# Two operands in one tile in a transformer FFN's down product, and the output projection's weight loads ordered ahead

## The chip, the core and the metric

The program runs on one core of one Trainium2 chip. A core has five engines that work side by side, each on its own queue of instructions: TensorE (PE, matrix products, with its weight loads shown as PEld), VectorE (DVE), ScalarE (ACT), GpSimd (POOL) and SyncE (SP), whose queue here issues most of the transfers between HBM and the on-chip memory SBUF. Products land in PSUM, a small memory of eight banks.

The metric is the device time of one execution in microseconds (us). The profile is of one execution; the times are of others.

## The reference, cut to what matters

A trunk of two layers on 1024 tokens of width 1024 in float32. The first layer mixes tokens by attention, the second by a recurrence; each then has a gated FFN of inner width 2816.

```python
x = x + mix
h = rms_norm(x, norm_ffn[layer])
x = x + swiglu(h, ffn_w_gate[layer], ffn_w_up[layer], ffn_w_down[layer])

def swiglu(h, w_gate, w_up, w_down):
    return (jax.nn.silu(h @ w_gate) * (h @ w_up)) @ w_down
```

The change touches the last product of the FFN, `(...) @ w_down`, in both layers, and in the attention layer the projection at the end of the mix, `concatenate([out_a, out_b]) @ w_out`, where `out_b` is a softmax-weighted sum of three attention patterns.

## The kernel before

**Float32 products from rounded parts.** TensorE multiplies a rounded form of float32 here. Each operand is split into a high part, written by ScalarE (a CAST), and a low part, source minus high part, written by VectorE: `split`, L153 and L154. A product of two operands is three matmuls, high by high, high by low and low by high.

**The FFN's down product** (`ffn_down`, from L893) is cut into blocks by Strassen's scheme in Winograd's form: the tokens in two halves of 512, the output columns in two halves of 512, the inner 2816 in two halves of 11 blocks of 128 (`N` is 11). The eight products of halves become seven, each a sum over `f` of 0 to 10. In the order of the program they are: the first and the second (plain operands), then the fifth and the sixth together, whose operands are sums of loaded blocks, then the third, the seventh and the fourth. One `f` of one product is two operands of 128 x 512 (a block of activations `act`, loaded from HBM, and one of `w_down`), two splits, and 12 matmuls (`add`, L932): four groups of 128 tokens, three matmuls each.

Before the change each operand has a tile of its own: `load` (L907 to L909) takes one of 12 `raw` tiles of 128 x 512 and issues one transfer; `halves` splits activations into `as` and weights into `ws`, five tiles of each. The blocks that the second product loads are kept in `s2[f]` and `t2[f]`; the fifth and sixth overwrite them with their own operands, which the third, seventh and fourth use again.

For each `f` of the fifth and sixth: GpSimd adds two activation blocks (L977), subtracts the kept weights from new ones (L978) and, after the split of the fifth's operands, subtracts the kept activations (L980); VectorE subtracts once (L981). Then the results, the sixth's operands, are split. TensorE takes the sixth's 12 matmuls of `f` after the fifth's 12 of `f + 1`.

In the third, seventh and fourth GpSimd makes one subtraction for each `f` (L993, L998, L1004) and in the seventh VectorE makes one more (L999). `to` (L938) adds a finished bank of PSUM to the residual.

**The output projection** (`out_proj`, called for the attention layer first) takes eight weight blocks `w[k]` for each half of the columns; each is loaded and split by `load_split` (the transfer is L168), with two `raw` tiles. Between the matmuls of blocks 0, 1 and 2 the program runs a part of `merge`: the first part reads the attention's statistics (L586) and a selector (L599) and turns them into weights of the three patterns; the other two load the patterns' outputs `oB` (L622), multiply them by those weights on VectorE (L625), add them on GpSimd (L627) and split the sum into the activations that the last two weight blocks need. The outputs of the last pattern are written to `oB` by GpSimd's queue (L513).

**What sets the order.** The program text gives dependencies and a priority, not the order of issue. The framework plans each engine's queue by a modelled timeline, in which an instruction is placed when the model has it ready; each engine then runs its queue strictly in that order, waiting where data is late. `after(ins, earlier)` adds an edge that fixes an order of issue and no wait. `seen` uses it to hold TensorE's instructions in the program's order in the projection of the first half of the tokens.

The functions that the diff touches, with what calls them:

Of the kernel before, what the change touches and what calls it, by code (L numbers as in the profile page):

```python
# [122 lines left out]
class Trunk:  # L123
# [144 lines left out]
    def attention(self, hp, mp):  # L268
# [333 lines left out]
        def merge(mp, psum, q, seen):  # L602
# [15 lines left out]
            for pr in range(2):  # L618
                yield
                l = ls[3 * pr:3 * pr + 3]  # L620
                for g in range(3):
                    nc.sync.dma_start(l[g], oB[g, pr][:, q * H:(q + 1) * H])  # L622
                    pb = psum.tile([P, H], F32, name="pb", tag="pd")
                    seen(nc.tensor.matmul(pb, selr[:, (g * 2 + pr) * P:(g * 2 + pr + 1) * P], f, start=True, stop=True))
                    nc.vector.tensor_tensor(l[g], pb, l[g], MUL)  # L625
                    if g:
                        nc.gpsimd.tensor_tensor(l[0], l[0], l[g], ADD)  # L627
                self.split(os2[q][1][:, 2 + pr, 0], os2[q][1][:, 2 + pr, 1], l[0])
# [264 lines left out]
    def ffn_down(self, layer, act, x_src, side, done):  # L893
# [5 lines left out]
        ve, po = nc.vector, nc.gpsimd  # L899
        es = ExitStack()  # L900
        pool = lambda n, b, **k: es.enter_context(TP(tc, name=n, bufs=b, **k))
        pr, xp, ap, bp, pk = (pool(n, 1, side=side) for n in ("dr", "dx", "da", "db", "dk"))
        py, pz = pool("fpa", 4, space=PSUM), pool("fpb", 4, space=PSUM)
        N = NF // 2
        inner = lambda j, f: f if j else N + f

        def load(src, keep=None):  # L907
            r = keep or pr.tile([P, H], F32, name="raw", tag="raw", bufs=12)
            nc.sync.dma_start(r, src)  # L909
            return r  # L910

        def A(q, j, f, keep=None):
            return load(act[inner(j, f), q], keep)

        def B(j, c, f, keep=None):
            return load(a["wd"][layer, inner(j, f)][:, c * H:(c + 1) * H], keep)

        def halves(s, w):
            r = []
            for p, n, z in ((ap, "as", s), (bp, "ws", w)):  # L920
                r.append(p.tile([P, 2, H], F32R, name=n, tag=n, bufs=5))
                self.split(r[-1][:, 0], r[-1][:, 1], z)
            return r

        banks = lambda p: [p.tile([P, H], F32, name="pd", tag="pd") for _ in range(4)]

        def add(ps, f, b, s, w, start):
            t = slice(b * P, (b + 1) * P)
            first = start and f == 0
            pe = nc.tensor.matmul  # L930
            for i, (x, y) in enumerate(((0, 0), (0, 1), (1, 0))):
                pe(ps[b], s[:, x, t], w[:, y], start=first and i == 0, stop=f == N - 1 and i == 2, skip_group_check=True)  # L932

        x = []

# [4 lines left out]
        def product(ps, start, take, ops, mid=None, last=2):  # L940

            end = []
            for f in range(N):
                o = halves(*ops(f))
                if f >= N - last:
                    end.append((f, o))
                    continue
                for b in range(4):
                    add(ps, f, b, *o, start)
                if mid and f == 4:  # L950
                    mid()
            for b in range(4):
                for f, o in end:
                    add(ps, f, b, *o, start)
                take(b)

        def load_x():
# [1 line left out]
                x.append(xp.tile([P, D], F32, name=f"x{b}"))  # L959
                nc.sync.dma_start(x[b], x_src[b * P:(b + 1) * P, :])  # L960

        s2, t2 = ([pk.tile([P, H], F32, name=f"{n}{f}") for f in range(N)] for n in ("s2", "t2"))
        zs, ys = banks(pz), banks(py)
        product(zs, True, lambda b: to(0, 0, zs, b), lambda f: (A(0, 1, f), B(1, 0, f)), load_x)
        product(ys, True, lambda b: to(0, 0, ys, b), lambda f: (A(0, 0, f, s2[f]), B(0, 0, f, t2[f])))
        zs = banks(pz)
        late = []

        def sixth(f, o):
            for b in range(4):  # L970
                add(ys, f, b, *o, False)
                if f == N - 1:
                    to(0, 1, ys, b)

        for f in range(N):
            s1, a22, t1, b22 = A(1, 0, f), A(1, 1, f), B(0, 1, f), B(1, 1, f)
            po.tensor_tensor(s1, s1, a22, ADD)  # L977
            po.tensor_tensor(t1, t1, t2[f], SUB)  # L978
            o5 = halves(s1, t1)
            po.tensor_tensor(s2[f], s1, s2[f], SUB)  # L980
            ve.tensor_tensor(t2[f], b22, t1, SUB)  # L981
            for b in range(4):
                add(zs, f, b, *o5, True)
                if f == N - 1:
                    to(1, 1, zs, b)
            late.append((f, halves(s2[f], t2[f])))
            if len(late) > 1:
                sixth(*late.pop(0))
        sixth(*late.pop())

        def third(f):
            a12, b22 = A(0, 1, f), B(1, 1, f)
            po.tensor_tensor(a12, a12, s2[f], SUB)  # L993
            return a12, b22

        def seventh(f):
            a22, b11 = A(1, 1, f), B(0, 0, f)
            po.tensor_tensor(a22, a22, s2[f], SUB)  # L998
            ve.tensor_tensor(b11, t2[f], b11, SUB)  # L999
            return a22, b11  # L1000

        def fourth(f):
            a22, b21 = A(1, 1, f), B(1, 0, f)
            po.tensor_tensor(b21, b21, t2[f], SUB)  # L1004
            return a22, b21

        def take3(b):
            to(0, 1, zs, b)
# [700 lines left out]
```

## Time and profile before

| what | value |
|---|---|
| time, median of 3 runs | 2815.28 us (2813.53 to 2815.95) |
| the profiled execution, its own time | 2819.46 us |
| span of the profile | 2817.7 us |
| mean granted TensorE clock | 0.963 |
| TensorE busy | 2648.6 us, 94% of the span |
| VectorE busy | 1739.9 us, 62% |
| ScalarE busy | 1198.0 us, 43% |
| GpSimd busy | 1053.6 us, 37% |
| down product of layer 0, first to last matmul | 1046.7 to 1277.1 us |
| down product of layer 1 | 2581.2 to 2807.3 us |
| output projection of layer 0 | 499.1 to 609.5 us |

A busy share is over the whole program. A stage of it can hang on another engine than the rest, so the stages are read one by one: in the views by group, an engine's idle time stands with the instruction that ended it, as `[idle <- releaser]`. "SPq", "POOLq" and the like are the queues that issue transfers. PEclk is the share of its full clock that TensorE was granted.

### The profile page before, as it was taken

The numbers are of one execution on the slowest core, as the hardware profiler recorded it, in microseconds if no ns is written. First come the engines' busy times: TensorE is split into PE (matmuls) and PEld (weight loads), VectorE is DVE, ScalarE is ACT, GpSimd is POOL, SyncE is SP. The second block draws the span as 40 slices with busy tenths as digits, with TensorE's granted clock in tenths as the row PEclk, the third lists the DMA queues.
The fourth block names the chain that finished last, engine by engine and source line by source line (L and its number), as shares of the span: only waits on it lengthen the run. The fifth ranks groups of instructions, "written<-read, shape, count | busy, mean of one in ns | idle before, by whom it ended". The sixth has DMA issues, their size and how long they took to land.

```text
span 2817.7 us, 42321 instructions
## 1 busy us (share of the span) xinstructions
PE 2648.6 (94%) x15526; PEld 2117.2 (75%) x15526; DVE 1739.9 (62%) x2961; ACT 1198.0 (43%) x2387; POOL 1053.6 (37%) x768
## 2 busy tenths in 40 slices
PE   8999998989999999998899889889899999999998
PEld 7777776677888877776677657678877888887776
DVE  4555565566344447888767677766677544444988
ACT  3445446334333333355644454334434333333334
POOL 1221221236434425545444433224444534441644
PEclk9999999999999999999999999888899999999999
DMA  4111112632222237463667588898552322225654
GB/s 140 46 38 46 46 53 73 216 111 82 83 86 86 79 115 254 152 202 112 215 201 206 148 245 214 216 253 247 180 195 86 105 79 87 79 69 204 206 157 161
DMA packets 304751, 392.61 MB, mean 139 GB/s; under 512 B 97928, under 2 KB 167944, under 8 KB 304544
## 3 DMA queue, kind: packets, MB, share of 16 engines
q1 hardware_dynamic: 299568, 375.72, 42.6%
q10 hardware_dynamic: 4496, 12.62, 1.1%
q8 instruction: 122, 2.00, 0.3%
q0 software_dynamic: 480, 1.57, 0.2%
q14 instruction: 85, 0.70, 0.1%
HBM read 281.56 MB, written 108.27 MB: 138 GB/s over the span
## 4 chain that ended last, share of the span: by engine, by line
PE 55%; DVE 14%; DMA 6%; issue 3%; POOL 2%; ACT 1%; SPq 1%; POOLq 0%; DVEq 0%; ACTq 0%
PE y L784 17%; PE z L784 9%; PE pd L932 6%; PE x L784 4%; PE pg L1360 2%; DVE ws L154 2%; DVE as L154 2%; PE pz L180 2%; PE pz L182 2%; PE pz L181 2%; PE o L1474 2%; DMA raw<-in_wd 2%; PE po L180 2%; PE po L181 1%; PE po L182 1%
## 5 line engine op out<-in xcount | busy, mean ns | idle before, releaser
L932 PE MATMUL pd<-ws,as 128*128 128x512 f32 x1848 | 431.9, 395 | 21.4 <-DVE ws L154 20.3
L932 PEld LDWEIGHTS pd<-ws,as 128*128 128x128 f32 x1848 | 350.7, 191 | 100.6 <-DVE ws L154 25.4
L784 PE MATMUL y<-t,cw 128*128 128x512 f32 x1584 | 370.2, 389 | 0.0
L784 PEld LDWEIGHTS y<-t,cw 128*128 128x128 f32 x1584 | 297.3, 188 | 62.4
L154 DVE TENSOR_TENSOR cw<-raw,cw 128x512 fp32r<-128x512 f32 x264 | 213.5, 811 | 201.6 <-ACT cw L154 198.0
L154 ACT CAST cw<-raw 128x512 fp32r<-128x512 f32 x264 | 163.1, 621 | 245.8 <-PE z L784 103.8
L793 POOL TENSOR_TENSOR c<-c 128x512 f32<-128x512 f32 x66 | 111.7, 1692 | 187.7 <-DVE c L800 136.7
L154 ACT CAST wh<-raw 128x512 fp32r<-128x512 f32 (+1 forms) x122 | 93.3, 766 | 173.5 <-PE mm L181 53.6
L180 PE MATMUL mm<-hx,wh 128*128 128x512 f32 x384 | 163.8, 427 | 0.0
L154 DVE TENSOR_TENSOR wl<-raw,wh 128x512 fp32r<-128x512 f32 (+1 forms) x114 | 110.4, 970 | 84.4 <-ACT wh L154 81.6
L788 ACT COPY sn<-y 128x512 f32<-128x512 f32 x132 | 76.9, 586 | 196.4 <-PE y L784 193.1
L182 PE MATMUL mm<-hx,wl 128*128 128x512 f32 x384 | 152.3, 397 | 0.0
L181 PE MATMUL mm<-hx,wh 128*128 128x512 f32 x384 | 151.6, 395 | 0.0
L784 PE MATMUL z<-b,cw 128*128 128x512 f32 x576 | 142.8, 399 | 6.6 <-DVE tx L730 6.6
L784 PEld LDWEIGHTS z<-b,cw 128*128 128x128 f32 x576 | 111.0, 193 | 31.1 <-issue 7.0
L154 ACT CAST as<-raw 128x512 fp32r<-128x512 f32 x110 | 68.2, 620 | 153.7 <-PE pd L932 80.1
L264 POOL TENSOR_TENSOR ry<-ry,S 128x512 f32<-128x512 f32 x40 | 51.7, 1293 | 217.3 <-DVE ry L263 192.8
L784 PE MATMUL y<-b,cw 128*128 128x512 f32 x528 | 129.0, 394 | 0.0
L784 PE MATMUL z<-t,cw 128*128 128x512 f32 x528 | 123.4, 389 | 0.0
L784 PE MATMUL x<-b,cw 128*128 128x512 f32 x480 | 116.4, 397 | 0.0
L784 PEld LDWEIGHTS y<-b,cw 128*128 128x128 f32 x528 | 98.8, 187 | 22.7
L826 POOL TENSOR_TENSOR raw<-s,raw 128x512 f32<-128x512 f32 x44 | 58.9, 1339 | 151.9 <-DVE cw L154 151.7
(464 smaller groups left out, 6091.8 us busy)
## 6 DMA issues: line engine op xcount, KB each, us to landing
raw<-act SPq DMA_DIRECT2D x132, 256.0 KB, 3.1
raw<-in_wd SPq DMA_DIRECT2D x132, 256.0 KB, 2.9
raw<-in_wg SPq DMA_DIRECT2D x88, 256.0 KB, 2.7
raw<-in_wu SPq DMA_DIRECT2D x88, 256.0 KB, 2.7
act<-c SPq DMA_DIRECT2D x88, 256.0 KB, 2.0
raw<-in_wrk SPq DMA_DIRECT2D x32, 512.0 KB, 4.8
raw<-in_win SPq DMA_DIRECT2D x24, 512.0 KB, 3.5
raw<-in_wout SPq DMA_DIRECT2D x32, 256.0 KB, 3.5
```

What stands on the lines that cost most here:

```text
L154: return self.nc.scalar.copy(hi, src), (eng or self.nc.vector).tensor_tensor(lo, src, hi.bitcast(F32), SUB)
L180: seen(mm(ps, lh, rh, start=start, stop=False))
L181: seen(mm(ps, lh, rl, start=False, stop=False))
L182: seen(mm(ps, ll, rh, start=False, stop=stop))
L264: nc.gpsimd.tensor_tensor(y, y, self.S[:, s], MUL)
L784: seen(pe.matmul(ps, w[:, x, s], bs[:, k, y], start=start and k == j == 0, stop=k == 3 and j == 2, skip_group_check=True))
L788: ac.copy(s, ps)
L793: po.tensor_tensor(g, g, u, MUL)
L826: po.tensor_tensor(a11, s, a11, SUB)
L932: pe(ps[b], s[:, x, t], w[:, y], start=first and i == 0, stop=f == N - 1 and i == 2, skip_group_check=True)
L1360: pe.matmul(ps[:, i], bk[rows, h * 4 + i].rearrange("p x t -> p (x t)"), ar[rows, h * 4 + i].rearrange("p y t -> p (y t)"), start=True, st ...
L1474: own(pe.matmul(*x, **k, skip_group_check=True))
```

## The change

In `ffn_down` one tile of 128 x 2 x 512 holds both operands of a product side by side: six `raw` tiles instead of twelve, `kept[f]` instead of `s2[f]` and `t2[f]`, and one `as` tile with the high and low parts of both operands instead of `as` and `ws`. Each operand is still a transfer of its own, into its half of the tile. A split is one CAST and one subtraction over 1024 columns instead of two of each over 512. In the fifth and sixth the three sums of each `f` that GpSimd made are made by VectorE, which thus makes all four; the sums of the third, seventh and fourth stay where they were. The number and the order of the matmuls are the same.

In `merge`, for the first half of the tokens, each load of `oB` is given an edge behind `self.splits[0]`, the transfer of the weight block that `load_split` loaded last.

```diff
--- before.py
+++ after.py
@@ -619,7 +619,9 @@
                 yield
                 l = ls[3 * pr:3 * pr + 3]
                 for g in range(3):
-                    nc.sync.dma_start(l[g], oB[g, pr][:, q * H:(q + 1) * H])
+                    load = nc.sync.dma_start(l[g], oB[g, pr][:, q * H:(q + 1) * H])
+                    if q == 0:
+                        self.after(load, self.splits[0])
                     pb = psum.tile([P, H], F32, name="pb", tag="pd")
                     seen(nc.tensor.matmul(pb, selr[:, (g * 2 + pr) * P:(g * 2 + pr + 1) * P], f, start=True, stop=True))
                     nc.vector.tensor_tensor(l[g], pb, l[g], MUL)
@@ -899,37 +901,34 @@
         ve, po = nc.vector, nc.gpsimd
         es = ExitStack()
         pool = lambda n, b, **k: es.enter_context(TP(tc, name=n, bufs=b, **k))
-        pr, xp, ap, bp, pk = (pool(n, 1, side=side) for n in ("dr", "dx", "da", "db", "dk"))
+        pr, xp, ap, pk = (pool(n, 1, side=side) for n in ("dr", "dx", "da", "dk"))
         py, pz = pool("fpa", 4, space=PSUM), pool("fpb", 4, space=PSUM)
         N = NF // 2
         inner = lambda j, f: f if j else N + f
 
-        def load(src, keep=None):
-            r = keep or pr.tile([P, H], F32, name="raw", tag="raw", bufs=12)
-            nc.sync.dma_start(r, src)
+        A = lambda q, j, f: act[inner(j, f), q]
+        B = lambda j, c, f: a["wd"][layer, inner(j, f)][:, c * H:(c + 1) * H]
+
+        def load(s, w, keep=None):
+
+            r = keep or pr.tile([P, 2, H], F32, name="raw", tag="raw", bufs=6)
+            for i, src in enumerate((s, w)):
+                nc.sync.dma_start(r[:, i], src)
             return r
 
-        def A(q, j, f, keep=None):
-            return load(act[inner(j, f), q], keep)
-
-        def B(j, c, f, keep=None):
-            return load(a["wd"][layer, inner(j, f)][:, c * H:(c + 1) * H], keep)
-
-        def halves(s, w):
-            r = []
-            for p, n, z in ((ap, "as", s), (bp, "ws", w)):
-                r.append(p.tile([P, 2, H], F32R, name=n, tag=n, bufs=5))
-                self.split(r[-1][:, 0], r[-1][:, 1], z)
+        def halves(z):
+            r = ap.tile([P, 2, 2, H], F32R, name="as", tag="as", bufs=5)
+            self.split(r[:, 0], r[:, 1], z)
             return r
 
         banks = lambda p: [p.tile([P, H], F32, name="pd", tag="pd") for _ in range(4)]
 
-        def add(ps, f, b, s, w, start):
+        def add(ps, f, b, z, start):
             t = slice(b * P, (b + 1) * P)
             first = start and f == 0
             pe = nc.tensor.matmul
             for i, (x, y) in enumerate(((0, 0), (0, 1), (1, 0))):
-                pe(ps[b], s[:, x, t], w[:, y], start=first and i == 0, stop=f == N - 1 and i == 2, skip_group_check=True)
+                pe(ps[b], z[:, x, 0, t], z[:, y, 1], start=first and i == 0, stop=f == N - 1 and i == 2, skip_group_check=True)
 
         x = []
 
@@ -941,17 +940,17 @@
 
             end = []
             for f in range(N):
-                o = halves(*ops(f))
+                o = halves(ops(f))
                 if f >= N - last:
                     end.append((f, o))
                     continue
                 for b in range(4):
-                    add(ps, f, b, *o, start)
+                    add(ps, f, b, o, start)
                 if mid and f == 4:
                     mid()
             for b in range(4):
                 for f, o in end:
-                    add(ps, f, b, *o, start)
+                    add(ps, f, b, o, start)
                 take(b)
 
         def load_x():
@@ -959,50 +958,50 @@
                 x.append(xp.tile([P, D], F32, name=f"x{b}"))
                 nc.sync.dma_start(x[b], x_src[b * P:(b + 1) * P, :])
 
-        s2, t2 = ([pk.tile([P, H], F32, name=f"{n}{f}") for f in range(N)] for n in ("s2", "t2"))
+        kept = [pk.tile([P, 2, H], F32, name=f"k{f}") for f in range(N)]
         zs, ys = banks(pz), banks(py)
-        product(zs, True, lambda b: to(0, 0, zs, b), lambda f: (A(0, 1, f), B(1, 0, f)), load_x)
-        product(ys, True, lambda b: to(0, 0, ys, b), lambda f: (A(0, 0, f, s2[f]), B(0, 0, f, t2[f])))
+        product(zs, True, lambda b: to(0, 0, zs, b), lambda f: load(A(0, 1, f), B(1, 0, f)), load_x)
+        product(ys, True, lambda b: to(0, 0, ys, b), lambda f: load(A(0, 0, f), B(0, 0, f), kept[f]))
         zs = banks(pz)
         late = []
 
         def sixth(f, o):
             for b in range(4):
-                add(ys, f, b, *o, False)
+                add(ys, f, b, o, False)
                 if f == N - 1:
                     to(0, 1, ys, b)
 
         for f in range(N):
-            s1, a22, t1, b22 = A(1, 0, f), A(1, 1, f), B(0, 1, f), B(1, 1, f)
-            po.tensor_tensor(s1, s1, a22, ADD)
-            po.tensor_tensor(t1, t1, t2[f], SUB)
-            o5 = halves(s1, t1)
-            po.tensor_tensor(s2[f], s1, s2[f], SUB)
-            ve.tensor_tensor(t2[f], b22, t1, SUB)
+            z, y, k = load(A(1, 0, f), B(0, 1, f)), load(A(1, 1, f), B(1, 1, f)), kept[f]
+            ve.tensor_tensor(z[:, 0], z[:, 0], y[:, 0], ADD)
+            ve.tensor_tensor(z[:, 1], z[:, 1], k[:, 1], SUB)
+            o5 = halves(z)
+            ve.tensor_tensor(k[:, 0], z[:, 0], k[:, 0], SUB)
+            ve.tensor_tensor(k[:, 1], y[:, 1], z[:, 1], SUB)
             for b in range(4):
-                add(zs, f, b, *o5, True)
+                add(zs, f, b, o5, True)
                 if f == N - 1:
                     to(1, 1, zs, b)
-            late.append((f, halves(s2[f], t2[f])))
+            late.append((f, halves(k)))
             if len(late) > 1:
                 sixth(*late.pop(0))
         sixth(*late.pop())
 
         def third(f):
-            a12, b22 = A(0, 1, f), B(1, 1, f)
-            po.tensor_tensor(a12, a12, s2[f], SUB)
-            return a12, b22
+            z = load(A(0, 1, f), B(1, 1, f))
+            po.tensor_tensor(z[:, 0], z[:, 0], kept[f][:, 0], SUB)
+            return z
 
         def seventh(f):
-            a22, b11 = A(1, 1, f), B(0, 0, f)
-            po.tensor_tensor(a22, a22, s2[f], SUB)
-            ve.tensor_tensor(b11, t2[f], b11, SUB)
-            return a22, b11
+            z = load(A(1, 1, f), B(0, 0, f))
+            po.tensor_tensor(z[:, 0], z[:, 0], kept[f][:, 0], SUB)
+            ve.tensor_tensor(z[:, 1], kept[f][:, 1], z[:, 1], SUB)
+            return z
 
         def fourth(f):
-            a22, b21 = A(1, 1, f), B(1, 0, f)
-            po.tensor_tensor(b21, b21, t2[f], SUB)
-            return a22, b21
+            z = load(A(1, 1, f), B(1, 0, f))
+            po.tensor_tensor(z[:, 1], z[:, 1], kept[f][:, 1], SUB)
+            return z
 
         def take3(b):
             to(0, 1, zs, b)
```

## The prediction

> **What bounds the kernel now.** First the page: the engines, the granted clock in slices, and the costliest group.
>
> ```profile
> PE 2648.6 (94%) x15526; PEld 2117.2 (75%) x15526; DVE 1739.9 (62%) x2961; ACT 1198.0 (43%) x2387; POOL 1053.6 (37%) x768
> PEclk9999999999999999999999999888899999999999
> L932 PE MATMUL pd<-ws,as 128*128 128x512 f32 x1848 | 431.9, 395 | 21.4 <-DVE ws L154 20.3
> ```
>
> TensorE is busy almost throughout, so the change can only give back time in which TensorE waits or runs at a lower clock. The down product's matmuls (L932) waited 21.4 us in both layers together, nearly all for VectorE's low part of the weights. Where that happened the timeline of TensorE says; the first five lines are layer 0, the others layer 1. The bracket is the idle time before.
>
> ```profile
> 1104.53 13.26 PE L932 MATMUL pd<-ws,as 128*128 128x512 f32 x57 [0.86 <-DVE ws L154]
> 1123.22 19.42 PE L932 MATMUL pd<-ws,as 128*128 128x512 f32 x72 [5.44 <-DVE ws L154]
> 1142.99 5.73 PE L932 MATMUL pd<-ws,as 128*128 128x512 f32 x24 [0.35 <-DVE ws L154]
> 1151.20 29.08 PE L932 MATMUL pd<-ws,as 128*128 128x512 f32 x127 [2.48 <-DVE ws L154]
> ...
> 2638.79 13.24 PE L932 MATMUL pd<-ws,as 128*128 128x512 f32 x57 [0.19 <-DVE ws L154]
> 2655.91 19.41 PE L932 MATMUL pd<-ws,as 128*128 128x512 f32 x72 [3.88 <-DVE ws L154]
> 2678.02 7.35 PE L932 MATMUL pd<-ws,as 128*128 128x512 f32 x24 [2.70 <-DVE ws L154]
> 2686.42 13.89 PE L932 MATMUL pd<-ws,as 128*128 128x512 f32 x60 [1.05 <-DVE ws L154]
> ```
>
> All eight gaps lie in or just ahead of the fifth and sixth products (about 1105 to 1170 and 2640 to 2704). Idle: 0.86 + 5.44 + 0.35 + 2.48 = 9.13 us and 0.19 + 3.88 + 2.70 + 1.05 = 7.82 us. The row of 127 gives 29.08 / 127 = 0.229 us a matmul. Rows that follow a long gap are slower: 19.42 for 72 is 2.93 too much, 19.41 is 2.92, 7.35 for 24 is 1.85: together 7.7 us. The windows of 1 us show why, the clock being the column before the last two:
>
> ```profile
> 1122.00:1123.00 1.00, 0.00 (x0) 0.72 0.80 213
> 1128.00:1129.00 1.00, 1.00 (x4) 0.50 0.90 307
> 2679.00:2680.00 1.00, 1.00 (x4) 0.50 0.83 215
> ```
>
> Idle and low clock together cost 9.13 + 7.82 + 7.7 = **24.65 us**. Why VectorE is late shows in its timeline beside GpSimd's:
>
> ```profile
> 1104.40 0.68 DVE L981 TENSOR_TENSOR t<-raw 128x512 f32<-128x512 f32 x1
> 1105.00 0.68 DVE L154 TENSOR_TENSOR as<-raw,as 128x512 fp32r<-128x512 f32 x1
> ...
> 1119.25 1.71 POOL L978 TENSOR_TENSOR raw<-raw,t 128x512 f32<-128x512 f32 x1
> 1119.76 1.74 DVE L154 TENSOR_TENSOR as<-raw,as 128x512 fp32r<-128x512 f32 x1
> ...
> 1120.92 1.70 POOL L980 TENSOR_TENSOR s<-raw,s 128x512 f32<-128x512 f32 x1
> 1121.43 1.74 DVE L154 TENSOR_TENSOR ws<-raw,ws 128x512 fp32r<-128x512 f32 x1
> ```
>
> Alone, VectorE starts such an instruction every 0.60 us (1104.40 to 1105.00). Beside GpSimd both take turns, one pair every 1.67 us (1119.76 to 1121.43). An `f` of the two products has five such VectorE instructions and three of GpSimd: three pairs and two alone make 3 x 1.67 + 2 x 0.60 = 6.21 us, against 24 x 0.229 = 5.50 us of TensorE. So here VectorE and GpSimd together are the bound.
>
> The second place is the start of the output projection, in the order of SP's queue (the last row is TensorE's):
>
> ```profile
> 484.84 0.37 SPq L586 DMA_DIRECT2D mtmp<-st  x1
> 485.26 0.57 SPq L622 DMA_DIRECT2D om<-oB  x1
> 485.88 0.80 SPq L599 DMA_DIRECT2D sel<-in_sel  x2
> 486.73 7.83 SPq L622 DMA_DIRECT2D om<-oB  x4
> 494.66 0.89 SPq L168 DMA_DIRECT2D raw<-in_wout  x2
> 498.40 0.62 ACT L154 CAST wh<-raw 128x512 fp32r<-128x512 f32 x1 [10.23 <-DMA raw<-in_wout]
> 499.07 0.79 PE L180 MATMUL po<-wh,o 128*128 128x512 f32 x1 [12.63 <-ACT wh L154]
> ```
>
> TensorE stands for 12.63 us until the first weight block has come, and its load stands in SP's queue behind four loads of `oB`. The waits of that queue name what held them, the last pattern's output on its way to HBM:
>
> ```profile
> SPq L622 <- DMA oB<-ob: 6.2, 1, 6.2
> ```
>
> **The change, part by part.**
>
> *The wide split.* The nearest rows are the splits over 1024 columns before 460 us, by group and in the timeline:
>
> ```profile
> L154 ACT CAST wh<-raw 128x1024 fp32r<-128x1024 f32 x19 | 19.9, 1045 | 48.2 <-PE mm L181 46.6 <-issue 1.6
> 31.72 1.21 DVE L154 TENSOR_TENSOR wl<-raw,wh 128x1024 fp32r<-128x1024 f32 x1
> 32.85 0.68 DVE L154 TENSOR_TENSOR hx<-tr,hx 128x512 fp32r<-128x512 f32 x1
> ```
>
> VectorE needs 32.85 - 31.72 = 1.13 us for what cost 2 x 0.60, ScalarE 1.05 for two CASTs of 0.62 each. In the plain products this saves nothing on the path, as TensorE has no gap there. A wide CAST must wait for both loads, and the first product of a layer starts with 0 to 1.2 us more or less for it; I take 0, because one long CAST is done about when the second short one was.
>
> *The sums.* Three go to VectorE at 0.60 each, if they run as the subtraction at L981 does, with nothing of GpSimd beside them; that holds, as all its work of this stage is gone. The other end is 1.67 each, as beside GpSimd. I take 0.60, since only the third product's sums can still overlap, at the stage's tail. VectorE then has 4 x 0.60 + 2 x 1.13 = 4.66 us for each `f`, under TensorE's 5.50; in `f`s the slack is 0.84. ScalarE has 2.10. What is late next is TensorE itself. The five `as` tiles hold two and a half `f`, as before, 2.5 x 5.50, so a late load has about 13 us of cover; if that cover is gone, VectorE's slack repays it only at 0.84 for each `f`. I leave 1 us of gaps in each layer: 24.65 - 2 = **22.6 us** gained, with 12 and 25 as ends.
>
> *The third, seventh and fourth* keep GpSimd's subtraction. VectorE now takes a turn of 1.13 rather than two of 0.60 against it, so no more in sum, and TensorE, the first number behind the length of the window, was busy almost to the end of it: 0.
>
> ```profile
> 1151.00:1213.00 62.00, 61.80 (x273) 51.19 (x274) 51.97 (x65) 23.67 (x41) 26.20 (x18) 1.00 0.52 158
> ```
>
> *The weights ahead.* With the loads of `oB` behind the transfers of blocks 1 and 2, SP issues L586, then the selector, then the first block: 484.84 + 0.37 + 0.05 + 0.80 + 0.05, about 486.1 instead of 494.66. Their memory is free by then: the first blocks lie where the attention's masks lay, whose last reader ends at 481.2.
>
> ```profile
> 480.93 0.28 DVE L465 CUSTOM_DVE_ANT_0 pr<-sc,masks 128x128 f32<-128x128 f32 x1
> ```
>
> So the path to the first matmul moves up by 494.66 - 486.1 = **8.5 us**, to 490.6. Behind the load of `oB` that waits until 494.2 there now stands block 2: it lands 3.7 us after 494.7 (as 494.66 to 498.40) and is split by 499.1. Ahead of block 2 TensorE has block 0 at half clock, eight small matmuls, block 1 and these three of `merge`:
>
> ```profile
> 508.71 0.96 PE L624 MATMUL pb<-mf,selr 44*128 44x512 f32 x3
> ```
>
> From 499.07 to 509.67 that was 10.6 us, so block 2 is needed at 501.2. Its cover is 2 us; if that is gone, the excess is lost. The `oB` data, issued at 494.3, land at about 498 if they take as long as block 0 did, ahead of their first use. The bounds of this part are 0, if the plan puts the weights no earlier, and 11.4: 8.5 and the half clock of this stretch, which is now at 500 to 504.7, if the shorter gap of 4.1 us escapes it.
>
> ```profile
> 490.00:491.00 1.00, 0.00 (x0) 0.99 0.83 240
> 491.00:492.00 1.00, 0.00 (x0) 0.50 1.06 418
> ```
>
> Before, the clock fell 4.6 us after the idle began at 486.4; a restart at 490.6 is too close to call, and I count nothing. [...]
>
> **The sum.** 22.6 + 8.5 = 31.1 us from the profiled execution's own 2819.46 (span 2817.7 and 1.8 around it). The median of the runs is 2815.28, 4.2 lower; taken from it, 2815.28 - 31.1 = **2784**.
>
> **The rivals.**
>
> *The projection does not gain.* The planner may set the weights where they were and push `oB` behind them, or block 2 and the `oB` loads come late and give the lead back. For it: SP's order is strict and L622's wait of 6.2 us stays. Against: the cover above. Time: 2815.28 - 22.6 = 2793.
>
> *VectorE stays the bound by half.* The transfers of both halves of a tile, the release of a pair only when its last reader is done, or an order that meets loads late, leave gaps; halves of 24.65 remain. For it: 85% use of VectorE is near the edge, and the third's GpSimd work runs into the tail. Against: no pair with GpSimd is left in between. Time: 2815.28 - 12.3 - 8.5 = 2794; with the first rival 2803.
>
> *VectorE waits for ScalarE (slower).* Both wide splits of an `f` need a CAST of 1.05 us first. If VectorE's queue has them straight behind the sums that they depend on, as the program is written, it stands for 1.05 twice: 4.66 + 2.10 = 6.76 us for each `f`, 1.26 above TensorE, over 22 `f` 27.7 us. Such gaps of 1 to 3 us also bring the half clock, as the one of 2.70 did at 1.85; one for every second `f` is 20 us. Then 2815.28 + 27.7 + 20 - 24.65 - 8.5 = 2830; it is slower than before from about 6 us for each `f` with these dips, or 7 without. Against: in the old queue other work fills that time, L981 of one `f` ahead of the split of another. [...]
>
> *The change does not do what it says*: if the two loads into one tile were made to follow each other, every pair would wait for two landings. The selector's two loads into one tile above are issued back to back, so I give this 1 in 100 and no range.
>
> **How the numbers follow.** Chances: both parts as forecast 0.55 (2776 to 2790); the projection without gain 0.15 (2790 to 2798); half of the FFN's, with or without the projection, 0.17 (2792 to 2805); VectorE waiting for ScalarE 0.08 (2815 to 2845); nothing measurable, by both parts failing, 0.04; the serial loads 0.01. The low end takes 11.4 instead of 8.5 and the last 2 us of gaps with 2 at the starts, about 2777; the high end reaches into the third case's upper half: 2777 to 2803 leaves out about 0.2. What a measurement can tell from no change is about 0.2%, 5.6 us. Faster by more: 0.55 + 0.15 + 0.17 less a little = 0.86; within 0.06; slower 0.08.
>
> **What would show it.** Right: between the first matmul at L932 and the third product no idle row above 1 us; windows of the fifth and sixth without GpSimd, VectorE at about 85% and clock 1.00; splits 128 x 1024 at 1.05 and 1.2 us; the first L168 on SP ahead of all L622 by `oB`, and the first matmul of the projection about 490.6. Wrong: idle rows of L932 ended by ScalarE or by loads, VectorE rows of 1.7 us in that stage without GpSimd beside them, or a matmul of block 2 waiting for its weights as long as the first did before.

## The result, and the profile after

| | before | after |
|---|---|---|
| median of the runs side by side | 2815.61 us (2813.53 to 2826.61) | 2785.81 us (2784.99 to 2786.05) |
| ratio, 95% interval | | 0.9881 [0.9861, 0.9901] |
| profiled execution, its span | 2817.7 us | 2784.0 us |

The forecast was 2784, in 2777 to 2803. The total agrees; its two parts do not, and that is what the rest is about. First the page of after, the engines and the costliest groups:

```profile
PE 2639.8 (95%) x15526; PEld 2114.8 (76%) x15526; DVE 1687.8 (61%) x2873; ACT 1183.5 (43%) x2233; POOL 947.3 (34%) x702
...
L931 PE MATMUL pd<-as 128*128 128x512 f32 x1848 | 421.8, 390 | 2.7 <-ACT as L154 1.2
```

The idle time of the down product's matmuls fell from 21.4 to 2.7 us. TensorE's timeline of after, layer 0 and then layer 1 (the last number ahead of a bracket is the count, the bracket is idle time before):

```profile
1044.49 1.19 PE L931 MATMUL pd<-as 128*128 128x512 f32 x4 [1.18 <-ACT as L154]
1046.60 155.35 PE L931 MATMUL pd<-as 128*128 128x512 f32 x684 [0.91 <-DVE as L154]
...
2563.85 209.30 PE L931 MATMUL pd<-as 128*128 128x512 f32 x920 [0.17 <-DVE as L154]
```

After the start there is one row of 684 matmuls in layer 0 and one of 920 in layer 1: no gap is left in the fifth and sixth products. The pitch is (155.35 - 0.39) / 683 = 0.2269 us, 0.39 being the one matmul that is shown whole. What the stage lost can now be told without adding up brackets: from the first start to the last there are 923 pitches, and 923 x 0.2269 are 209.4 us. The source view gives the first and the last start:

```profile
L931 PE MATMUL pd<-as x924: 388/389/499, 1044.5 to 1260.4; 128*128 128x512 f32 x185
```
```profile
L931 PE MATMUL pd<-as x924: 387/389/505, 2561.8 to 2772.8; 128*128 128x512 f32 x185
```

That is 215.9 and 211.0 us, against 230.4 and 226.1 before: a gain of 14.5 + 15.1 = **29.6 us**, where 22.6 were forecast. Losses above 209.4 fell from 21.0 and 16.7 to 6.5 and 1.6.

Windows of the fifth and sixth in both layers (sum, TensorE, its loads, VectorE, ScalarE, GpSimd, clock, transfers, GB/s), and two groups of VectorE and ScalarE in the part from 1088 to 1134:

```profile
1088.00:1149.00 61.00, 61.00 (x271) 50.52 (x270) 55.11 (x67) 23.11 (x22) 7.25 (x4) 1.00 0.58 181
2607.00:2668.00 61.00, 61.00 (x270) 50.53 (x270) 54.23 (x66) 24.03 (x23) 8.16 (x5) 1.00 0.55 179
```
```profile
L154 DVE TENSOR_TENSOR as<-k,as 128x1024 fp32r<-128x1024 f32 x10 | 12.2, 1219 | 0.0
...
L154 ACT CAST as<-raw 128x1024 fp32r<-128x1024 f32 x8 | 8.4, 1053 | 12.8 <-PE pd L931 12.8
```

TensorE is busy for all 61 us at full clock; ScalarE's CASTs wait for TensorE to release a tile (`PE pd`), the sign that VectorE and ScalarE run ahead. Up to 1134 VectorE waits for no CAST. From 1139 on it does, up to 1.50 us, but its splits then come every 2.72 us, the pace of 12 matmuls: it waits for ScalarE, and ScalarE for TensorE. VectorE is busy for 55.11 of the 61 us, 90% where about 85% was forecast, and GpSimd is not absent: four subtractions of the third product lie in this window. Why VectorE is not held up before 1134, its timeline says:

```profile
1108.72 1.22 DVE L154 TENSOR_TENSOR as<-raw,as 128x1024 fp32r<-128x1024 f32 x1
1109.85 0.69 DVE L980 TENSOR_TENSOR k<-raw 128x512 f32<-128x512 f32 x1
1110.45 0.69 DVE L977 TENSOR_TENSOR raw<-raw,k 128x512 f32<-128x512 f32 x1
1111.06 0.69 DVE L979 TENSOR_TENSOR k<-raw,k 128x512 f32<-128x512 f32 x1
1111.66 1.22 DVE L154 TENSOR_TENSOR as<-k,as 128x1024 fp32r<-128x1024 f32 x1
```

Sums start every 0.60 us and a wide split takes 1109.85 - 1108.72 = 1.13, both as forecast: 4.66 us for an `f`. The split at 1111.66 starts as soon as the sum at L979 is out of the way, 0.60 us after that began, so it cannot be the split of that sum, which has a CAST of 1.05 us ahead of it. It is an earlier `f`'s: the planner has put work of other `f`s between a sum and its own split, and the CASTs run beside that.

The projection went the other way. Its first matmul is early by the whole forecast, and two waits follow that before did not have:

```profile
490.59 0.50 PE L180 MATMUL po<-wh,o 128*128 128x512 f32 x1 [3.23 <-ACT wh L154]
...
502.47 0.50 PE L180 MATMUL po<-wh,o 128*128 128x512 f32 x1 [1.73 <-ACT wh L154]
...
517.73 0.50 PE L180 MATMUL po<-wh,o 128*128 128x512 f32 x1 [1.56 <-ACT wh L154]
...
608.68 7.51 PE L786 MATMUL y<-b,cw 128*128 128x512 f32 x32
```
```profile
610.21 6.12 PE L784 MATMUL y<-b,cw 128*128 128x512 f32 x26
```

The second fence is before: there FFN-up began at 610.21. The lead at the start was 499.07 - 490.59 = 8.5 us, at the end 610.21 - 608.68 = **1.5 us**. Both places also carry what came before them: the attention's last matmul ended at 486.43 before and at 487.36 here, and from that end to FFN-up it is 123.8 us before and 121.3 after, 2.5 less. The windows from the first projection matmul to FFN-up, before and then after, say where it went:

```profile
499.00:610.20 111.20, 105.17 (x444) 80.95 (x445) 63.02 (x87) 36.06 (x61) 33.11 (x27) 0.96 0.51 171
```
```profile
490.50:608.70 118.20, 107.94 (x445) 82.55 (x446) 63.05 (x89) 35.97 (x61) 33.80 (x29) 0.94 0.53 183
```

Idle time is 118.20 - 107.94 = 10.3 us against 6.0: 4.2 more. The clock is lower, 0.94 for 0.96: lost 0.06 x 118.2 = 7.1 us against 0.04 x 111.2 = 4.4, 2.7 more. Together 6.9 of the 7.0 us by which the stretch grew. By windows of 1 us, some 1.7 us of the clock's loss follow the second wait (518 to 522). About as much more than before is lost at 566 to 573, behind a wait of 4.08 us for a norm that stands in both kernels and not behind these loads, and about 1.1 us less at the start. SP's queue and the chain of waits name the loads:

```profile
487.22 0.83 SPq L168 DMA_DIRECT2D raw<-in_wout  x2
488.09 7.10 SPq L622 DMA_DIRECT2D om<-oB  x3
495.30 1.05 SPq L687 DMA_DIRECT2D x<-in_x  x2
496.45 0.37 SPq L168 DMA_DIRECT2D raw<-in_wout  x1
...
511.44 0.80 SPq L622 DMA_DIRECT2D om<-oB  x2
512.34 0.38 SPq L168 DMA_DIRECT2D raw<-in_wout  x1
```
```profile
496.45 5.33 DMA raw<-in_wout
...
512.34 4.62 DMA raw<-in_wout
```

Block 2 was issued not at 494.7 but at 496.45, behind two loads of `x` (512 KB each), and took 5.33 us where the first block had taken 3.7. The last weight block of the column half stood behind two `oB` loads of the *second* column half, which have no edge.

### The profile page after: what moved, and what is told of

The parts are those of the page before. It is cut to its first block, busy times and chain, and to the rows that moved or that the text cites. A ratio compares the mean times of both kernels' runs of the same rounds, so it can differ in the third digit from the quotient of the medians.

```text
span 2784.0 us, 41818 instructions
## 1 busy us (share of the span) xinstructions
PE 2639.8 (95%) x15526; PEld 2114.8 (76%) x15526; DVE 1687.8 (61%) x2873; ACT 1183.5 (43%) x2233; POOL 947.3 (34%) x702
## 4 chain that ended last, share of the span: by engine, by line
PE 75%; DVE 10%; DMA 6%; issue 3%; ACT 3%; POOL 1%; SPq 1%; POOLq 0%; DVEq 0%; ACTq 0%
PE y L786 17%; PE pd L931 12%; PE z L786 9%; PE mm L180 4%; PE x L786 4%; PE mm L182 3%; PE mm L181 3%; PE pz L180 2%; PE pz L182 2%; PE o L1473 2%; PE pz L181 2%; PE pg L1359 2%; PE po L181 1%; PE po L180 1%; PE po L182 1%
## 5 line engine op out<-in xcount | busy, mean ns | idle before, releaser
L931 PE MATMUL pd<-as 128*128 128x512 f32 x1848 | 421.8, 390 | 2.7 <-ACT as L154 1.2
L931 PEld LDWEIGHTS pd<-as 128*128 128x128 f32 x1848 | 346.1, 188 | 76.6 <-DVE as L154 2.4
L154 ACT CAST as<-raw 128x1024 fp32r<-128x1024 f32 x110 | 114.3, 1052 | 158.5 <-PE pd L931 103.9
L154 DVE TENSOR_TENSOR as<-raw,as 128x1024 fp32r<-128x1024 f32 x110 | 149.3, 1373 | 51.1 <-ACT as L154 48.3
```

The source lines that it names most:

```text
L154: return self.nc.scalar.copy(hi, src), (eng or self.nc.vector).tensor_tensor(lo, src, hi.bitcast(F32), SUB)
L931: pe(ps[b], z[:, x, 0, t], z[:, y, 1], start=first and i == 0, stop=f == N - 1 and i == 2, skip_group_check=True)
```

## The experiments

Eleven kernels ran in three sets, each beside runs of before on the same chip; the medians of before were 2820.3 us (20 runs, 2810.7 to 2828.6), 2818.0 (9 runs) and 2817.6 (13 runs). "Length" is the time from the first to the last start of the down product's matmuls, layer 0 and layer 1: 230.4 and 226.1 before, 215.9 and 211.0 after.

**Without the edge.** Does the projection contribute?

```diff
-                    load = nc.sync.dma_start(l[g], oB[g, pr][:, q * H:(q + 1) * H])
-                    if q == 0:
-                        self.after(load, self.splits[0])
+                    nc.sync.dma_start(l[g], oB[g, pr][:, q * H:(q + 1) * H])
```

> The whole change without the edge on the loads of oB (the FFN's part alone). Theory A, that the projection's lead is mostly lost again before the FFN (first matmul 8.5 us earlier, the FFN's first matmul only 1.5 us earlier): 2787 to 2789 us, some 2 us above the changed kernel's 2785.8. Rival, as the prediction summed it, that the edge is worth 8.5 us and the FFN the remaining 21: about 2794 us.

2788.66 us (2786.39 to 2788.92), ratio 0.9893 [0.9873, 0.9913], lengths 216.6 and 211.2. The FFN's part alone gives all but some 3 us, less than the intervals can tell apart.

**The edge alone**, on the kernel before:

```diff
-                    nc.sync.dma_start(l[g], oB[g, pr][:, q * H:(q + 1) * H])
+                    load = nc.sync.dma_start(l[g], oB[g, pr][:, q * H:(q + 1) * H])
+                    if q == 0:
+                        self.after(load, self.splits[0])
```

> The kernel before with the edge alone. Theory A (lead lost again): 2812 to 2814 us, 1 to 3 us under before's 2815.6, with the projection's first matmul at about 490.6 and a gap ahead of block 2 and of the last block as in the changed kernel. Rival (the edge is worth its 8.5 us): 2807 us.

2818.5 us (2809.99 to 2827.13), ratio 1.0003 [0.9989, 1.0017], lengths 230.1 and 227.5. The times show no difference. So the forecast gain of 8.5 us is not there, with or without the FFN's part. The same two waits stand in TensorE's timeline of this kernel:

```profile
502.31 0.50 PE L180 MATMUL po<-wh,o 128*128 128x512 f32 x1 [1.52 <-ACT wh L154]
...
517.70 0.49 PE L180 MATMUL po<-wh,o 128*128 128x512 f32 x1 [1.67 <-ACT wh L154]
```

**The sums back on GpSimd**, everything else as changed:

```diff
-            ve.tensor_tensor(z[:, 0], z[:, 0], y[:, 0], ADD)
-            ve.tensor_tensor(z[:, 1], z[:, 1], k[:, 1], SUB)
+            po.tensor_tensor(z[:, 0], z[:, 0], y[:, 0], ADD)
+            po.tensor_tensor(z[:, 1], z[:, 1], k[:, 1], SUB)
             o5 = halves(z)
-            ve.tensor_tensor(k[:, 0], z[:, 0], k[:, 0], SUB)
+            po.tensor_tensor(k[:, 0], z[:, 0], k[:, 0], SUB)
```

> The changed kernel with the three sums of the fifth and sixth products back on GpSimd, the tiles still paired. Theory C, that VectorE and GpSimd taking turns are the bound: 3 x 1.07 of GpSimd's turns + 0.60 + 2 x 1.13 of VectorE's = 6.07 us for each f against TensorE's 5.50, so gaps ended by VectorE and half clock come back, 12 to 22 us in both layers: 2798 to 2808 us. Rival W, that the wide split is what helped: 2786 us, no gap.

2803.16 us (2795.62 to 2810.61), ratio 0.9943 [0.9923, 0.9963], lengths 225.3 and 221.0. The gaps are back in TensorE's timeline, and VectorE's shows the turns:

```profile
1139.26 5.75 PE L931 MATMUL pd<-as 128*128 128x512 f32 x24 [0.43 <-DVE as L154]
1145.42 5.74 PE L931 MATMUL pd<-as 128*128 128x512 f32 x24 [0.41 <-DVE as L154]
```
```profile
1120.48 1.77 DVE L980 TENSOR_TENSOR k<-raw 128x512 f32<-128x512 f32 x1
1122.18 2.31 DVE L154 TENSOR_TENSOR as<-k,as 128x1024 fp32r<-128x1024 f32 x1
1124.42 1.21 DVE L154 TENSOR_TENSOR as<-raw,as 128x1024 fp32r<-128x1024 f32 x1
```

An `f`, 24 matmuls, now takes 1145.42 - 1139.26 = 6.16 us. The same wide split takes 2.31 us with a turn of GpSimd ahead of it and 1.21 without. GpSimd's own row beside the longer one (L979) runs from 1121.78 to 1123.41; the split begins at 1122.18 and ends at 1124.49, 1.08 us after GpSimd, which is about the 1.13 of a split alone. Pairing still brought 15 us over the edge alone (2818.5 to 2803.2), of which the lengths show 11. One wide split meets one turn of GpSimd where two short ones met two, but that this is the reason is not shown: 6.16 us for an `f` is hardly less than the 6.21 that the prediction summed for separate tiles.

**The sums on VectorE, operands in separate tiles** (the kernel before with the edge and these lines):

```diff
-            po.tensor_tensor(s1, s1, a22, ADD)
-            po.tensor_tensor(t1, t1, t2[f], SUB)
+            ve.tensor_tensor(s1, s1, a22, ADD)
+            ve.tensor_tensor(t1, t1, t2[f], SUB)
             o5 = halves(s1, t1)
-            po.tensor_tensor(s2[f], s1, s2[f], SUB)
+            ve.tensor_tensor(s2[f], s1, s2[f], SUB)
```

> The kernel before (one tile for each operand, narrow splits) with the edge and with the three sums on VectorE. Theory C: VectorE alone needs 8 x 0.60 = 4.80 us for each f, under 5.50, so the stage is fed: 2785 to 2790 us. Rival W, that the pairing is needed: gaps stay, 2800 us or more.

2788.12 us (2784.73 to 2790.74), ratio 0.9892 [0.9868, 0.9915], lengths 215.6 and 214.8. In the fifth and sixth products TensorE runs without a gap; the first row is layer 0, the others layer 1:

```profile
1053.39 127.00 PE L934 MATMUL pd<-ws,as 128*128 128x512 f32 x559 [1.11 <-DVE ws L154]
...
2566.46 169.79 PE L934 MATMUL pd<-ws,as 128*128 128x512 f32 x741 [1.32 <-DVE ws L154]
2736.80 19.33 PE L934 MATMUL pd<-ws,as 128*128 128x512 f32 x84 [0.56 <-DVE ws L154]
2756.61 21.83 PE L934 MATMUL pd<-ws,as 128*128 128x512 f32 x95 [0.47 <-DVE ws L154]
```

So moving the sums is what counts most: alone it is worth 30 us (2818.5 to 2788.1), pairing alone 15, both together some 33. They are two cures of one bound and do not add. Pairing's own share beside the moved sums, 2 to 3 us, lies within the intervals of the times, but the rows show it: in layer 1 the gaps of 1.32, 0.56 and 0.47 us, outside the fifth and sixth, are there with single tiles and not with paired ones, and the length is 214.8 instead of 211.0.

**VectorE's queue in the order of the text**, for the rival that VectorE waits for ScalarE. `low` collects the low-part subtractions of the splits:

```diff
+            before = low[-1]
+            for ins in (ve.tensor_tensor(z[:, 0], z[:, 0], y[:, 0], ADD),
+                        ve.tensor_tensor(z[:, 1], z[:, 1], k[:, 1], SUB)):
+                self.after(ins, before)
             o5 = halves(z)
+            for ins in (ve.tensor_tensor(k[:, 0], z[:, 0], k[:, 0], SUB),
+                        ve.tensor_tensor(k[:, 1], y[:, 1], z[:, 1], SUB)):
+                self.after(ins, low[-1])
```

> The changed kernel with VectorE's queue held to the order of the program text in the fifth and sixth products: edges (an order, no wait) put the two sums of the sixth's operands behind the low part of the fifth's split, and the next f's first two sums behind the low part of the sixth's. Nothing is left out. Theory (the planner's order is what hid the two CASTs): VectorE now stands for a CAST of 1.05 us and its hand-over twice per f, so an f takes about 4.66 + 2.10 = 6.8 us or a little more instead of 5.45, over 20 f some 25 to 30 us, and gaps of 1 us or more bring the half clock in places: 2810 to 2830 us, with idle rows of TensorE in these products ended by VectorE and idle of VectorE ended by the CAST. Rival (VectorE has enough slack, or the order is the text's already): within 3 us of the changed kernel, no idle rows above 0.5 us.

2825.34 us (2816.45 to 2837.1), ratio 1.0025 [1.0003, 1.0047], lengths 238.8 and 231.5. VectorE's timeline, and windows of the same stretch:

```profile
1128.42 1.23 DVE L154 TENSOR_TENSOR as<-raw,as 128x1024 fp32r<-128x1024 f32 x1 [1.19 <-ACT as L154]
...
1135.66 1.23 DVE L154 TENSOR_TENSOR as<-raw,as 128x1024 fp32r<-128x1024 f32 x1 [1.19 <-ACT as L154]
```
```profile
1134.00:1164.00 30.00, 27.55 (x102) 17.60 (x101) 19.90 (x25) 8.84 (x9) 1.06 (x1) 1.00 0.47 155
```

An `f` takes 1135.66 - 1128.42 = 7.24 us: 4.66, two waits of 1.19 and some hand-over. The same instructions in another order on one queue turn a gain of 30 us into a loss. The rival's time of 2830 was near, but for another reason: its price for an `f` was 6.76, and its 20 us of half clock did not come, as the clock is 1.00 from 1088 to 1180 and from 2560 to 2760; gaps of about 0.25 us, of which there is one for every 12 matmuls here, did not lower it.

**The other subtractions on VectorE too** (third, seventh, fourth):

```diff
-            po.tensor_tensor(z[:, 0], z[:, 0], kept[f][:, 0], SUB)
+            ve.tensor_tensor(z[:, 0], z[:, 0], kept[f][:, 0], SUB)
```

> The changed kernel with GpSimd's subtractions of the third, seventh and fourth products on VectorE as well, so that VectorE has no partner in the whole down product. Theory C: the changed kernel's TensorE has no gap in these products, so nothing is left to gain: within 2 us of the changed kernel, with VectorE's wide splits all at 1.22 us instead of a mean of 1.37. Rival: taking turns still costs TensorE something there, 3 us or more are gained.

2780.93 us (2779.43 to 2785.26), ratio 0.9871 [0.9854, 0.9888], lengths 214.2 and 212.0. The median is 4.3 us below that of the changed kernel in the same set, whose second measurement follows. That is the rival's size, but the intervals overlap. The profile speaks for theory C: the two lengths together are 426.2 us against 426.9, though the wide splits of loaded operands do fall from a mean of 1.37 to 1.24 us over both layers.

> The changed kernel once more, as the yardstick for the runs of this set: 0.988 of before; from the end of the attention's last matmul to the first of the FFN's up product about 121 to 124 us (before 123.8).

2785.2 us (2777.55 to 2787.98), ratio 0.9879 [0.9859, 0.9899]. From the end of the attention's last matmul to FFN-up this profile has 119.9 us, less than the 121 to 124 expected. The same stretch is 123.8 before and 125.3 without the edge, 121.3 in the first profile of the changed kernel and 119.6 with the edge alone. So the edge is worth some 2 to 6 us there, more than the 1.5 of one pair of profiles; 8.5 is out of reach in all of them.

**Edges on all late loads.** If the lead was lost to loads that slipped ahead of the weights, holding those back should return it:

```diff
                     load = nc.sync.dma_start(l[g], oB[g, pr][:, q * H:(q + 1) * H])
-                    if q == 0:
-                        self.after(load, self.splits[0])
+                    self.after(load, self.splits[0])
...
-                            nc.sync.dma_start(x[b], x_src[b * P:(b + 1) * P, :])
+                            xl = nc.sync.dma_start(x[b], x_src[b * P:(b + 1) * P, :])
+                            if merge and h == 0:
+                                self.after(xl, self.splits[0])
```

> The changed kernel with edges also on the loads of oB of the second column half and on the loads of x, so that those of x no longer stand ahead of block 2 nor those of oB ahead of the last block. Theory B, that the lead is lost to these loads on SP's queue and in the DMA engines: the gap of 1.56 us ahead of the last block goes and that of 1.73 ahead of block 2 shrinks; 2 to 5 us under the changed kernel. Rival D, that what follows the projection takes the lead back anyway: within 1 us of the changed kernel.

2774.22 us (2771.53 to 2778.74), ratio 0.9846 [0.9828, 0.9864]. SP's queue, the landing of block 2 from the chain of waits, TensorE's timeline and the window of the whole stretch:

```profile
495.12 0.37 SPq L168 DMA_DIRECT2D raw<-in_wout  x1
495.53 1.38 SPq L622 DMA_DIRECT2D om<-oB  x3
...
497.43 0.43 SPq L686 DMA_DIRECT2D x<-in_x  x1
```
```profile
495.12 3.20 DMA raw<-in_wout
```
```profile
500.46 0.96 PE L625 MATMUL pb<-mf,selr 44*128 44x512 f32 x3 [0.83 <-DVE mf L615]
...
504.87 1.69 PE L625 MATMUL pb<-mf,selr 44*128 44x512 f32 x3 [0.48 <-DVE om L626]
```
```profile
490.40:604.20 113.80, 105.46 (x445) 80.68 (x446) 63.81 (x88) 36.14 (x62) 33.82 (x29) 0.97 0.55 190
```

Block 2 goes out at 495.12, ahead of `x`, and lands in 3.20 us instead of 5.33. From there on no matmul waits for weights; what is left of waits in the first column half are 0.83 and 0.48 us inside `merge`. The stretch takes 113.8 us instead of 118.2, and FFN-up starts at 604.07 instead of 608.68: of the 7.0 us lost, 4.4 are back. (From the attention's end it is 116.9 us, 4.4 and 3.0 less than in the two profiles of the changed kernel.) The median fell by 11, more than the 2 to 5 expected.

**The loads of `oB` alone** (the first part of that diff):

> The changed kernel with the edge on the loads of oB of both column halves, but none on the loads of x. Nothing is left out. Theory A (the last block of the second column half behind the second half's loads of oB is what cost the lead there, the x loads cost block 2 its landing time): block 2 is still late by 1.5 to 2 us, the gap ahead of the last block is gone, so about half the gain of the edges together: 2778 to 2782 us. Theory B (the loads of x are the whole difference): 2783 to 2787. Theory C (the loads of oB are the whole of it): 2772 to 2776.

2780.84 us (2778.36 to 2783.49), ratio 0.9847 [0.9818, 0.9875]. TensorE's timeline:

```profile
503.51 0.79 PE L180 MATMUL po<-wh,o 128*128 128x512 f32 x1 [1.84 <-ACT wh L154]
...
520.10 0.51 PE L180 MATMUL po<-wh,o 128*128 128x512 f32 x1 [0.31 <-ACT wh L154]
```

As theory A had it: the wait ahead of the last block shrinks from 1.56 to 0.31 us, that of block 2 stays (1.84). So the first hangs on the `oB` loads and the second on the `x` loads. The time lies between the two others, though the intervals do not separate it from either, and the profile does not show the gain: from the attention's end to FFN-up it has 120.5 us. Here the half clock followed the gap ahead of block 2 (0.50 from 504 to 510).

**The parts of `merge` one block later**, against the waits of 0.83 and 0.48:

```diff
-                        if merged and k in ((0, 1, 2), (0, 1, 2))[c]:
+                        if merged and k in ((0, 2, 3), (0, 1, 2))[c]:
```

> As e7, and the two parts of merge that load oB come one weight block later, behind blocks 2 and 3, so that block 2 is issued ahead of every load of oB, as soon as its tile is free, at about 492 instead of 496.5. Theory B: no gap of TensorE between the first matmul and the end of the first column half; 4 to 7 us under the changed kernel. Rival D: within 1 us of it.

2774.81 us (2770.45 to 2784.36), ratio 0.9851 [0.9829, 0.9873]. The two waits are gone, but FFN-up starts at 603.83 instead of 604.07, and the time is that of the kernel with the edges alone.

**Edges and subtractions together:**

> Both additions together, on the changed kernel: edges behind the last weight load for all loads of oB and for the loads of x in the first half of the tokens, and the subtractions of the third, seventh and fourth products on VectorE instead of GpSimd. Nothing is left out. Theory (the two sit in different stages and add up): the edges alone gave 2774.2 and the subtractions alone about 4 us below the changed kernel's 2785.2, so 2768 to 2773 us. Rival (the subtractions' 4 us were spread between runs): 2772 to 2777 us, and the down product's length in the profile within 1 us of that with the edges alone (217.0 and 210.9 us from first to last matmul).

2770.79 us (2769.02 to 2776.07), ratio 0.9817 [0.9791, 0.9843], lengths 215.8 and 212.5. This is the fastest seen; each of its runs is below each run of the changed kernel. Against the edges alone it is 3 us less, which the intervals do not separate, and the lengths say nothing for it (1.2 us shorter and 1.6 longer).

## Why the prediction was right, and which steps failed

**The bound was named rightly.** Giving the sums back to GpSimd returns gaps, turns of 1.7 to 2.3 us and 6.16 us for an `f`; taking GpSimd out of the fifth and sixth removes every gap there, with paired or single operands.

**Durations held:** 0.60 for a sum, 1.13 for a wide split, 1.05 for its CAST, 4.66 us for an `f`.

**The gain of the FFN was too small in the sum.** The step was "I leave 1 us of gaps in each layer: 24.65 - 2 = 22.6". It measured 29.6, beyond its end of 25, so the 24.65 was short too. It summed the eight gaps near the fifth and sixth and put the wide split at nothing elsewhere: "In the plain products this saves nothing on the path, as TensorE has no gap there", and 0 for the third, seventh and fourth, read from a window of layer 0. These rows of TensorE's timeline of before, layer 1, were left out:

```profile
2583.92 54.68 PE L932 MATMUL pd<-ws,as 128*128 128x512 f32 x240 [1.32 <-DVE ws L154]
...
2766.03 19.34 PE L932 MATMUL pd<-ws,as 128*128 128x512 f32 x84 [0.43 <-DVE ws L154]
2785.83 21.87 PE L932 MATMUL pd<-ws,as 128*128 128x512 f32 x95 [0.47 <-DVE ws L154]
```

Of the 1.32, 0.17 remain after; the other two are gone: 1.15 + 0.43 + 0.47 = 2.05 us in this layer. It is the pairing that removes them: with the sums on VectorE and single tiles they stay, and with paired tiles and the sums on GpSimd TensorE runs from 2678.69 to the end without a gap. And a bracket is smaller than what its gap costs: a matmul is shown 0.39 us long where the next may start after 0.227, so each gap hides 0.16 us, 1.1 us for the seven gaps of layer 1 among these and the eight. Of the 16.7 us lost in layer 1 the sum had 7.82 + 2.92 + 1.85 = 12.6; these two make it 15.7, near the measured 16.7 - 1.6 = 15.1. In layer 0 the sum had 9.13 + 2.93 = 12.1 of 14.5. Its four gaps hide 0.65, and about 1.2 us less is lost where TensorE also runs the next layer's transposes (L211): 43 matmuls took 16.2 us there before (1216.6 to 1232.8) and 41 took 14.6 after (1201.6 to 1216.1), 6.4 and 5.3 more than at the pitch of 0.2269.

**The projection's step failed**: "Its cover is 2 us; if that is gone, the excess is lost." The start moved by the 8.5 us worked out, to 490.59 for 490.6. But block 2 was forecast at 494.7 with a landing of 3.7; the planner put the loads of `x` into the place that `oB` had left, so it was issued at 496.45 and took 5.33. And the end of the column half was not looked at: its last block met the second half's `oB` loads. The rival "the projection does not gain" (0.15) came nearly true, by the second of its two ways: 1.5 us of 8.5 are left in this pair of profiles, 2.5 counted from the attention's end, 3.9 in the second profile of the changed kernel. The experiments with edges show both loads as the cause of those waits; the half clock behind the second is shown by the windows.

**The total agreed by luck, since the errors cancelled**: +7.0 in the FFN, -7.0 in the projection. The two profiles differ by 33.7; the 2.6 beyond 29.6 + 1.5 lie between the two down products, from the last start of one to the first of the other: 2581.2 - 1277.1 = 1304.1 us before, 2561.8 - 1260.4 = 1301.4 after. Nothing was changed there, and single profiles of these kernels have 1288.6 to 1308.3.

**The other rivals.** "VectorE stays the bound by half" fell: no gap is left. "VectorE waits for ScalarE" fell by the planner's order, and is real without it: with the queue in the order of the text VectorE waits 1.19 us for each CAST, and an `f` takes 7.24 us.

**Open.** The edges shorten the projection by 3.0 to 4.4 us in the profiles, the medians fall by 11. Their profiled executions also have a higher mean clock (0.971 and 0.973 against 0.965), and a shorter stretch between the down products (1290.7 and 1288.6 us), which the edit does not touch. In the pages' three slices of about 69 us from about 1870 to 2080 the clock stands at 9, 9 and 9 tenths with the edges alone and at 8, 9 and 9 with both additions, against 8, 8 and 9 (from about 1880) in the changed kernel, which has 0.93 from 1900 to 2050; why was not settled.

## What to carry to other kernels

Where VectorE and GpSimd take turns, count the turns, not the busy times: an operation moved to VectorE can cost less there (0.60 us) than it did on GpSimd (a pair of 1.67), if VectorE's queue has other work to place beside the CASTs it depends on. Size a stage by its matmul count times the undisturbed pitch and subtract, instead of adding up the gaps that one sees, and do so for each layer: a window of one showed no gap where the other had them. A transfer that is held back opens a place in the queue: list what else is ready to take it, up to the end of the stage, and give the same edge to all of those.

## What the hardware showed that was not expected

The half clock came after a gap of only 1.56 us. In the changed kernel TensorE stood that long ahead of 517.73, and windows of 1 us show:

```profile
516.00:517.00 1.00, 0.17 (x1) 0.00 (x0) 0.00 (x0) 0.00 (x0) 0.00 (x0) 1.00 0.96 361
...
519.00:520.00 1.00, 1.00 (x4) 0.79 (x3) 0.32 (x1) 0.00 (x0) 0.00 (x0) 0.50 0.71 213
```

The idle began at 516.17; by 519 TensorE works again, at half clock. The gap of 1.73 us ahead of 502.47 in the same run did not lower it (1.00 from 500 to 507), while the one of 1.84 us ahead of 503.51 in the kernel with the edge on all loads of `oB` did (0.50 from 504). In before the longer gap of 2.48 us ahead of 1151.20 left it at 1.00 (1147 to 1157), so in these runs the length alone does not decide.

A weight block of 256 KB that landed in 3.7 us before, with the transfer engines busy for 0.75 of that time, took 5.33 us with 1 MB of `x` issued just ahead of it (0.96), and 3.20 us when the edge put `x` behind it: a landing time is no price for another place in the queue.
